# Half of the k-tiles of 25 tile pairs by Strassen's scheme, in a two-layer token-mixing network on one core

## The chip, the core and the metric

The kernel runs on one core of one Trainium2 chip. The metric is the device time of one execution in microseconds (us); less is better. The engines are PE (TensorE, matrix products), DVE (VectorE), ACT (ScalarE), POOL (GpSimd) and SP (SyncE, which starts most DMA transfers). SBUF is the on-chip memory of 128 partitions, PSUM the banks into which PE writes.

## What is computed

Two layers act on x, 512 tokens by 2048 features, in float32. Each is a norm, an input projection, two kinds of mixers over the tokens, and an output projection that is added to x:

```python
def even_layer(x, norm_g, w_in, ...):        # layer 0
    proj = rmsnorm(x, norm_g) @ w_in         # 2048 -> 9 x 1024 + 8 gates
    qa, ka, va, za, qb, kb, vb, ob, zb, gif = split_cols(proj, EV_SIZES)
    ya = chunk_rel_attention(qa, ka, va, ...) * silu(za)            # 8 heads of 128
    yb = sigmoid(ob) * mlstm_chunkwise(qb, kb, vb, li, lf) * silu(zb)   # 4 heads of 256
    return concatenate([ya, yb]) @ w_out
def odd_layer(x, ...):                       # layer 1
    xc, zc, qd, kd, vd, zd, a_pre, b_pre = split_cols(rmsnorm(x, norm_g) @ w_in, OD_SIZES)
    yc = rg_lru(causal_dwconv(xc), ...) * silu(zc)                  # 8 blocks of 128
    yd = rmsnorm(gated_delta_chunkwise(q, k, v, beta, g)) * silu(zd)    # 8 heads of 128
    return concatenate([yc, yd]) @ w_out
for layer in range(2):
    x = x + (even_layer if layer == 0 else odd_layer)(x, ...)
```

## The kernel before

Features lie on the partitions, in 16 k-tiles of 128, and the 512 tokens along the free dimension. Every float32 operand is the sum of a high and a low float32r part, and one product takes three passes (high by high L216, high by low L217, low by high L218), each a matmul of 128x128 weights against 128x512 tokens. One output tile of 128 features is thus 16 k-tiles by 3 passes, 48 matmuls into one of four PSUM banks named `pp`.

`tiles()` cuts an output tile into four units of four k-tiles; `tiles_tok()` makes units of one k-tile for projections that are wanted with tokens on the partitions (the values v), which hold all four `pp` banks at once (L256 to L258). `run()` goes through the units in order. Ahead of unit u it emits the loads up to u + 10 (on SP's queue, into `wr` tiles, of which there are `RAWS` = 4), the splits of the weights up to five units ahead (`AHEAD`; `split_weights`, ACT L185 makes the high part, DVE L186 the low part, into `act` slots, `SLOTS` = 28) and the splits of the operands up to three units ahead (`LEAD`):

```python
while self.nsplit < min(n, u + 1 + AHEAD):
    self.split_weights(self.nsplit)
    self.nsplit += 1
for v in range(u, min(n, u + 1 + LEAD)):
    self.operands(*self.units[v], v == u)
```

The mixers are generators. After every second k-tile `tick()` emits one step of each active one (three in layer 0), and a table of lags `LAG` says how many steps lie between what a mixer orders and what uses it. The order of the instructions on PE, DVE, ACT and POOL is the order in which the program emits them. A finished tile is evicted from PSUM by DVE with the row scale of the norm (L281, L283; L310 and L311 for the token products).

Layer 0 has a first group of five tiles and the gates, which advance together while x arrives (each k-tile of x is split by ACT L354 and DVE L355 or L352, and squared and summed by POOL), then 51 single tiles and four token products, ordered by head: k, q, (v), o, z of the four mLSTM heads, then k, q, (v), z of the eight attention heads (`ATTN_ORDER`), then the 16 output tiles. In an mLSTM head, `pk` holds a matrix of decays that POOL and ACT prepare (L607, L613) and DVE multiplies by the scores from PSUM (L631); POOL adds up its blocks (L634 to L637). The last score block is a product of unsplit operands. In an attention head ACT takes logarithm, exponential and square of the norms (L683, L685, L688, with loads of function tables between), and its last step puts the head's output z into `self.t`, from which the output projection takes it. In layer 1, L1083 and L1080 split the gate weights of a recurrent block.

Of the kernel before, what the change touches and what calls it, by code (L numbers as in the profile page):

```python
# [8 lines left out]
F32 = mybir.dt.float32  # L9
# [7 lines left out]
P = 128  # L17
# [17 lines left out]
# columns of the packed small parameters  # L35
# [28 lines left out]
class Net:  # L64
    """Both layers, features on partitions and tokens along the free dimension.

    Projections: each float32 operand is the exact sum of two float32r parts; a product
    takes three passes (high*high, high*low, low*high). Their weights are streamed in
    pieces of KW k-tiles. The mixers are generators; one step of each active one is
    emitted after every few products of the stream, so that what they wait for is there  # L70
    when the tensor engine comes to them.
    """

    def __init__(self, ctx, tc, a):
# [21 lines left out]
        # the clock of the tensor engine rises after a few microseconds of work  # L96
# [6 lines left out]
        self.t, self.x, self.raw = {}, {}, {}  # L103
        self.heads = 0

# [35 lines left out]
    def tiles(self, specs, group=1):  # L141
        """specs: (weights [P, 16, 128], act, done(psum)); `group` of them advance together.
# [1068 lines left out]
```

## Time and profile before

| | before |
|---|---|
| median of three runs | 1889.77 us (1888.33 to 1890.74) |
| the profiled execution: its span | 1888.7 us |
| PE busy | 1861.9 us, 99% |
| DVE, ACT, POOL busy | 1082.9, 753.1, 254.5 us |

The span of the profiled execution runs from its first to its last instruction; nothing beside the span is recorded of that execution's own time. The busy time of PE counts matmuls that overlap only once, and the mean duration of a matmul is longer than the distance from one to the next.

### The profile page before, as it was taken

To read this page: it belongs to the slowest core of one execution; us is meant where nothing else is said; L and a number is where in the kernel's file an instruction comes from. 1 tells how busy PE (TensorE), PEld (TensorE's weight loads), DVE (VectorE), ACT (ScalarE), POOL (GpSimd) and SP (SyncE) were. 2 spreads that over 40 slices of the span, in tenths; PEclk is the share of its full clock that TensorE was granted. 3 is DMA by queue.
4 is the path that set the end of the run, shared out by engine and by line. 5 is a ranking of instruction groups with operands and counts; after the bars stand their busy time and mean duration, and the time that the engine had idled before them with its cause. 6 is when DMAs were issued, how large, how long until landed. Compare 5 with 4: busy or idle time off the path is not lost.

```text
span 1888.7 us, 24074 instructions
## 1 busy us (share of the span) xinstructions
PE 1861.9 (99%) x8814; PEld 1526.8 (81%) x8814; DVE 1082.9 (57%) x1871; ACT 753.1 (40%) x1311; POOL 254.5 (13%) x298
## 2 busy tenths in 40 slices
PE   7999999999999999999999999999999999999999
PEld 5788888888888888888888788887788877778887
DVE  8564444334443655356643589989756666767222
ACT  4252323223243555355432544363324434566111
POOL 8110000000000011000121113400211112101000
PEclk9999999999999999999999999999999999999999
DMA  5333333333333332332454345433533334235432
GB/s 168 95 113 93 100 104 94 88 104 95 92 85 98 79 95 88 103 85 75 115 174 150 115 121 158 158 106 91 156 96 102 104 96 114 65 95 187 131 115 67
DMA packets 116694, 206.20 MB, mean 109 GB/s; under 512 B 21328, under 2 KB 22480, under 8 KB 116576
## 3 DMA queue, kind: packets, MB, share of 16 engines
q1 hardware_dynamic: 108512, 181.59, 33.8%
q0 software_dynamic: 5760, 18.88, 2.9%
q10 hardware_dynamic: 2304, 4.20, 0.6%
q8 instruction: 69, 1.13, 0.2%
q14 instruction: 49, 0.40, 0.1%
HBM read 189.37 MB, written 15.24 MB: 108 GB/s over the span
## 4 chain that ended last, share of the span: by engine, by line
PE 87%; DVE 8%; issue 2%; DMA 1%; ACT 1%; SPq 1%; DVEq 0%; POOL 0%; ACTq 0%; POOLq 0%
PE pp L216 23%; PE pp L218 23%; PE pp L217 23%; PE pp L256 3%; PE pp L258 3%; PE pp L257 3%; DVE act L186 2%; DVE ev L862 1%; DVE act L939 1%; DVE act L355 1%; DMA ev<-in_xT 1%; SPq L932 0%; PE at_tr L727 0%; PE inv_z L975 0%; ACT act L185 0%
## 5 line engine op out<-in xcount | busy, mean ns | idle before, releaser
L216 PE MATMUL pp<-act,act 128*128 128x512 f32 x2160 | 860.3, 398 | 1.1 <-ACT act L185 0.6
L218 PE MATMUL pp<-act,act 128*128 128x512 f32 x2160 | 846.8, 392 | 11.7 <-DVE act L186 11.5
L217 PE MATMUL pp<-act,act 128*128 128x512 f32 x2160 | 844.8, 391 | 1.6 <-DVE act L355 1.6
L186 DVE TENSOR_TENSOR act<-wr,act 128x512 fp32r<-128x512 f32 x608 | 440.0, 748 | 224.2 <-ACT act L185 223.4
L218 PEld LDWEIGHTS pp<-act,act 128*128 128x128 f32 x2160 | 407.0, 188 | 102.3 <-DVE act L186 15.6
L216 PEld LDWEIGHTS pp<-act,act 128*128 128x128 f32 x2160 | 407.7, 189 | 86.0 <-ACT act L185 2.5
L185 ACT ACTIVATE act<-wr 128x512 fp32r<-128x512 f32 x608 | 355.6, 621 | 302.2 <-DMA wr<-in_wi 117.3
L217 PEld LDWEIGHTS pp<-act,act 128*128 128x128 f32 x2160 | 407.9, 189 | 82.4 <-DVE act L355 3.1
L281 DVE TENSOR_TENSOR ev<-pp,rb 128x512 f32<-128x512 f32 x63 | 43.5, 690 | 154.7 <-PE pp L218 154.6
L256 PE MATMUL pp<-act,act 128*128 128x512 f32 x256 | 101.2, 395 | 0.0
L258 PE MATMUL pp<-act,act 128*128 128x512 f32 x256 | 99.9, 390 | 0.0
L257 PE MATMUL pp<-act,act 128*128 128x512 f32 x256 | 99.8, 390 | 0.0
L862 DVE SCALAR_TENSOR_TENSOR ev<-cv,cst,ev 128x512 f32<-128x512 f32 x96 | 85.3, 889 | 2.3
L456 ACT ACTIVATE tmp<-ev 128x512 f32<-128x512 f32 x56 | 34.8, 622 | 89.7 <-DVE ev L281 73.8
L716 POOL TENSOR_SCALAR pq<-pq,mx 128x512 f32<-128x512 f32 (+3 forms) x32 | 36.4, 1137 | 251.3 <-DVE mx L715 251.2
L800 DVE TENSOR_TENSOR ev<-ev,pp 128x512 f32<-128x512 f32 x16 | 11.0, 688 | 91.2 <-PE pp L218 91.2
L379 ACT ACTIVATE ev<-ev 128x512 fp32r<-128x512 f32 x40 | 25.2, 630 | 92.7 <-DVE ev L694 36.8
L258 PEld LDWEIGHTS pp<-act,act 128*128 128x128 f32 x256 | 48.1, 188 | 10.2
L256 PEld LDWEIGHTS pp<-act,act 128*128 128x128 f32 x256 | 48.1, 188 | 9.5
L257 PEld LDWEIGHTS pp<-act,act 128*128 128x128 f32 x256 | 48.1, 188 | 9.2
L560 ACT ACTIVATE tmp<-ev 128x512 f32<-128x512 f32 x15 | 9.5, 632 | 99.5 <-DVE ev L553 99.5
L553 DVE TENSOR_TENSOR ev<-ev,pp 128x512 f32<-128x512 f32 x16 | 11.0, 688 | 64.6 <-PE pp L218 54.3
(314 smaller groups left out, 1662.7 us busy)
## 6 DMA issues: line engine op xcount, KB each, us to landing
wr<-in_wi SPq DMA_DIRECT2D x416, 256.0 KB
wr<-in_wo SPq DMA_DIRECT2D x128, 256.0 KB
wr<-in_wv SPq DMA_DIRECT2D x64, 256.0 KB
tmp<-rows SPq DMA_DIRECT2D x24, 256.0 KB
ev<-in_xT SPq DMA_DIRECT2D x16, 256.0 KB
ev<-in_xT POOLq DMA_DIRECT2D x16, 256.0 KB, 3.1
x1d<-ev POOLq DMA_DIRECT2D x16, 256.0 KB, 2.3
ev<-x1d POOLq DMA_DIRECT2D x16, 256.0 KB, 4.4
```

Source lines behind the costliest of these rows:

```text
L185: nc.scalar.activation(h, w, AF.Copy)
L186: nc.vector.tensor_tensor(l, w, h.bitcast(F32), ALU.subtract)
L216: nc.tensor.matmul(ps, h[:, j, :], xh, start=k == 0, stop=False)
L217: nc.tensor.matmul(ps, h[:, j, :], xl, start=False, stop=False)
L218: nc.tensor.matmul(ps, l[:, j, :], xh, start=False, stop=k == KT - 1)
L256: nc.tensor.matmul(ps, xh, h, start=k == 0, stop=False)
L257: nc.tensor.matmul(ps, xh, l, start=False, stop=False)
L258: nc.tensor.matmul(ps, xl, h, start=False, stop=k == KT - 1)
L281: self.nc.vector.tensor_tensor(t, ps, self.rb, ALU.mult)
L456: nc.scalar.activation(th, t, AF.Tanh, scale=0.5)
L716: nc.gpsimd.tensor_scalar(s, s, mx[:, 3, b : b + 1], None, ALU.mult)
L862: nc.vector.scalar_tensor_tensor(t, cv[:, j : j + S], self.col(wcol + j), t, ALU.mult, ALU.add)
```

## The change

Of layer 0's 56 plain input tiles, six are now in the first group, and the other 50 form 25 pairs, which the list `STREAM0` orders. A pair takes k-tiles 0 to 7 by the Winograd form of Strassen's scheme and k-tiles 8 to 15 as before. The 2x2 blocks of the scheme are the pair's two output tiles by the even and odd k-tiles (weights), and even and odd k-tiles by the two halves of 256 tokens (x). Seven products of four k-tiles replace eight, so that 84 matmuls of 128x256 stand in place of 48 of 128x512, next to 48 of 128x512 that stay. A pair has eleven units instead of eight:

```diff
+    def pairs(self, specs):
+        for ws, wd, act, done in specs:
+            s = dict(kind="s", ws=ws, w=wd, act=act, done=done)
+            for f in ("1", "6", "7", "5", "2", "3", (0, 0), (0, 4), "4", (1, 0), (1, 4)):
+                self.units.append((s, f))
```

The sums and differences of weights that the scheme wants are made by POOL from the raw tiles ahead of the split (L221, L224), and each of the seven is then split as weights were (ACT L246, DVE L247):

```diff
+    def form(self, s, f):
+        sub = lambda o, x, y: nc.gpsimd.tensor_tensor(o, x, y, ALU.subtract)
+        if f == "6":
+            nc.gpsimd.tensor_tensor(s["a", 1], s["a", 1], s["a", 2], ALU.add)
+            sub(s["a", 0], s["a", 1], s["a", 0])
+        elif f == "7":
+            s["s3"] = self.raw_tile()
+            sub(s["s3"], s["a", 2], s["a", 0])
+            return s["s3"]
+        elif f == "3":
+            sub(s["a", 0], s["a", 3], s["a", 0])
```

The sums of x are made once, for four pairs of k-tiles, by `sums()`, which `operands()` calls when the first pair comes within three units: an ACT copy with the gain (L310), four DVE operations of 128x256 (L315, three L314), an ACT copy of 128x1024 (L320) and a DVE subtraction of 128x1024 (L321).

The partial results are put together in PSUM where the scheme allows it. Units 6 and 5 are followed by an ACT copy of a bank to SBUF (L352, tiles `ee`), unit 3 by three POOL adds of 128x256 (L355). The evictions add these to PSUM by halves: three half-width DVE operations for the first tile of a pair, two full ones for the second (L424 to L433):

```diff
+            if f in "65":
+                e = s["e" + f] = self.ep.tile([P, S], F32, tag="ee", name=self.uid("ee"), bufs=2)
+                nc.scalar.activation(e, ps, AF.Copy)
+            if f == "3":
+                e16, e75 = s["e6"], s["e5"]
+                add = lambda o, x, y: nc.gpsimd.tensor_tensor(o, x, y, ALU.add)
+                add(e75[:, H:], e16[:, :H], e75[:, H:])
+                add(e16[:, :H], e16[:, :H], e16[:, H:])
+                add(e16[:, H:], e16[:, :H], e75[:, :H])
```

A mixer's finished output goes to DRAM by a POOL DMA (`put()`, L492) where the loads have not yet come to the output projection, and SP loads it again. The buffers change; of `pk` and `pq` there is one tile each instead of two, the mLSTM heads take their turns one after the other (`mheads`), and the last mLSTM score block is now a product of split operands:

```diff
-SLOTS = 28
-EVS = 28
-TMPS = 6
-RAWS = 4
+SLOTS = 34
+EVS = 20
+TMPS = 5
+RAWS = 7
+    def put(self, act, k, t):
+        first = next(u for u, (s, _) in enumerate(self.units) if s["act"] == act)
+        if self.ndma < first:
+            self.nc.gpsimd.dma_start(self.yd[k], t)
+            self.spilt.add((act, k))
+        else:
+            self.t[act, k] = t
-                if n > P:
-                    kb, qb = [t[:, j * P : j * P + P] for t in kp[i]], [t[:, j * P :] for t in qp[i]]
-                    self.product(ps[:, :n], kb, qb, start=i == 0, stop=i == 1)
-                else:
-                    nc.tensor.matmul(ps[:, :n], k2[i][:, j * P : j * P + P], q2[i][:, j * P :], start=i == 0, stop=i == 1)
+                kb, qb = [t[:, j * P : j * P + P] for t in kp[i]], [t[:, j * P :] for t in qp[i]]
+                self.product(ps[:, :n], kb, qb, start=i == 0, stop=i == 1)
```

In the whole program there are 1200 matmuls of 128x512 less and 2100 of 128x256 more; POOL has 175 `TENSOR_TENSOR` and 25 DMAs more, SP 25 DMAs more.

Three places show how the order moves. The first is DVE at the end of the first token product; `pp128` is the first bank of the token product before, `pp138` after, and `ml_s` are mLSTM scores. Before:

```order
L814 TENSOR_SCALAR spl_1000<-sm178_997 128x8
L631 TENSOR_TENSOR pk169_942<-pk169_942,ml_s_180_1007 128x512
L186 TENSOR_TENSOR act182_1017<-wr156_885,act182_1017 128x512
L631 TENSOR_TENSOR pk169_942<-pk169_942,ml_s_183_1026 128x384
L631 TENSOR_TENSOR pk169_942<-pk169_942,ml_s_184_1040 128x256
L186 TENSOR_TENSOR act186_1050<-wr163_914,act186_1050 128x512
L311 SCALAR_TENSOR_TENSOR ev188_1057<-pp128_694,rcol_644,act187_1056 128x512
L311 SCALAR_TENSOR_TENSOR ev189_1063<-pp129_695,rcol_644,act187_1056 128x512
```

After, from the last of the four blocks of `sums()`:

```order
L315 TENSOR_TENSOR act200_1091<-tmp199_1089 128x256
L314 SCALAR_TENSOR_TENSOR act200_1091<-ev10_119,cst_77,act200_1091 128x256
L314 SCALAR_TENSOR_TENSOR act200_1091<-ev10_119,cst_77,tmp199_1089 128x256
L314 SCALAR_TENSOR_TENSOR act200_1091<-ev10_119,cst_77,act200_1091 128x256
L321 TENSOR_TENSOR act202_1097<-act200_1091,act201_1096 128x1024
...
L792 TENSOR_TENSOR pk178_1012<-pk178_1012,ml_s_205_1123 128x512
L247 TENSOR_TENSOR act207_1133<-wr162_923,act207_1133 128x512
L792 TENSOR_TENSOR pk178_1012<-pk178_1012,ml_s_208_1142 128x384
L792 TENSOR_TENSOR pk178_1012<-pk178_1012,ml_s_209_1156 128x256
L247 TENSOR_TENSOR act210_1164<-wr172_984,act210_1164 128x512
L468 SCALAR_TENSOR_TENSOR ev212_1171<-pp138_766,rcol_643,act211_1170 128x512
```

The eviction of the token product's first bank (L311, now L468) and the products with the scores (L631, now L792) have four blocks of five operations ahead of them, of which the first rows show the last.

The second is ACT in an attention head, around the logarithm and exponential of the norms. Before:

```order
L185 ACTIVATE act673_3976<-wr655_3891 128x512
L683 ACT_TABLE_LOAD
L683 ACTIVATE ev675_3988<-at_ss_657_3902,bc98_530 128x512
L683 ACTIVATE ev676_3989<-at_ss_674_3985,bc98_530 128x512
L685 ACT_TABLE_LOAD
L685 ACTIVATE ev675_3988<-ev675_3988 128x512
L685 ACTIVATE ev676_3989<-ev676_3989 128x512
L688 ACTIVATE tmp677_3994<-ev675_3988 128x512
L688 ACTIVATE tmp678_3995<-ev676_3989 128x512
L185 ACTIVATE act680_4006<-wr658_3911 128x512
L185 ACTIVATE act682_4026<-wr664_3935 128x512
```

After:

```order
L246 ACTIVATE act888_5649<-wr876_5569 128x512
L845 ACT_TABLE_LOAD
L845 ACTIVATE ev891_5670<-at_ss_874_5548,bc100_534 128x512
L845 ACTIVATE ev892_5671<-at_ss_890_5667,bc100_534 128x512
L847 ACT_TABLE_LOAD
L847 ACTIVATE ev891_5670<-ev891_5670 128x512
L847 ACTIVATE ev892_5671<-ev892_5671 128x512
L850 ACTIVATE tmp893_5676<-ev891_5670 128x512
L850 ACTIVATE tmp894_5677<-ev892_5671 128x512
L246 ACTIVATE act896_5683<-wr866_5494 128x512
L246 ACTIVATE act899_5701<-wr883_5612 128x512
L352 ACTIVATE ee900_5716<-pp897_5686 128x512
```

A copy of a bank of PSUM (L352, from the pair's bank `pp897`) now stands behind the run of table loads and activations and two splits.

The third is POOL in the mLSTM stage; `wr` are raw weights, `ee` the copies from PSUM. Before, what it did for two heads:

```order
L634 COPY tmp194_1087<-pk169_942 128x128
L635 TENSOR_TENSOR tmp194_1087<-pk169_942 128x384
L636 TENSOR_TENSOR tmp194_1087<-tmp194_1087,pk169_942 128x256
L637 TENSOR_TENSOR tmp194_1087<-tmp194_1087,pk169_942 128x128
L607 TENSOR_TENSOR tmp272_1544<-tmp271_1542,tri2_106 128x512
L610 MEMSET pk273_1546 128x128
L634 COPY tmp309_1786<-pk273_1546 128x128
L635 TENSOR_TENSOR tmp309_1786<-pk273_1546 128x384
L636 TENSOR_TENSOR tmp309_1786<-tmp309_1786,pk273_1546 128x256
L637 TENSOR_TENSOR tmp309_1786<-tmp309_1786,pk273_1546 128x128
```

After, what it does for one pair:

```order
L355 TENSOR_TENSOR ee279_1554<-ee272_1514,ee279_1554 128x256
L355 TENSOR_TENSOR ee272_1514<-ee272_1514 128x256
L355 TENSOR_TENSOR ee272_1514<-ee272_1514,ee279_1554 128x256
L224 TENSOR_TENSOR wr276_1535<-wr276_1535,wr277_1537 128x512
L221 TENSOR_TENSOR wr273_1516<-wr276_1535,wr273_1516 128x512
L221 TENSOR_TENSOR wr290_1649<-wr277_1537,wr273_1516 128x512
L221 TENSOR_TENSOR wr273_1516<-wr284_1606,wr273_1516 128x512
L492 DMA yd_101<-ev283_1604 128x512
```

Seven sums and a DMA for each pair stand where POOL had a few operations per head.

## Rows read from the trace of the kernel before

**Rows 1.** The page: span, busy time by engine, PE and DVE in 40 slices (tenths).

```profile
span 1888.7 us, 24074 instructions
PE 1861.9 (99%) x8814; PEld 1526.8 (81%) x8814; DVE 1082.9 (57%) x1871; ACT 753.1 (40%) x1311; POOL 254.5 (13%) x298
...
PE   7999999999999999999999999999999999999999
...
DVE  8564444334443655356643589989756666767222
```

**Rows 2.** Table by stage: window, length, PE, PEld, DVE, ACT, POOL busy (count), PEclk, DMA share, GB/s.

```profile
0.00:100.00 100.00, 86.94 (x364) 63.94 (x365) 71.63 (x72) 38.41 (x58) 47.72 (x39) 0.95 0.42 135
...
200.00:300.00 100.00, 100.00 (x455) 83.36 (x454) 41.85 (x66) 30.14 (x56) 4.73 (x7) 1.00 0.34 99
...
800.00:900.00 100.00, 100.00 (x463) 83.00 (x462) 57.78 (x116) 58.88 (x108) 9.35 (x8) 1.00 0.29 78
...
1100.00:1200.00 100.00, 100.00 (x486) 83.52 (x485) 92.50 (x221) 46.74 (x78) 32.61 (x43) 1.00 0.51 151
...
1300.00:1400.00 100.00, 95.17 (x507) 77.68 (x506) 70.40 (x99) 28.56 (x50) 12.54 (x16) 0.97 0.44 119
```

**Rows 3.** Timeline of PE: start us, us, engine, line, operation, out<-in; a stream of 512-wide products.

```profile
400.12 0.39 PE L216 MATMUL pp<-act,act 128*128 128x512 f32 x1
...
400.80 0.39 PE L216 MATMUL pp<-act,act 128*128 128x512 f32 x1
```

**Rows 4.** Timeline of PE: the first of six 256-wide products and the product behind them.

```profile
574.66 0.28 PE L387 MATMUL at_pv<-ev,act 128*128 128x256 f32 x1
...
575.37 0.40 PE L216 MATMUL pp<-act,act 128*128 128x512 f32 x1
```

**Rows 5.** Groups by line, whole span: count, busy us, mean ns, idle before and its releasers.

```profile
L185 ACT ACTIVATE act<-wr 128x512 fp32r<-128x512 f32 x608 | 355.6, 621 | 302.2 <-DMA wr<-in_wi 117.3 <-DVE ev L800 103.2 <-PE pp L218 42.1
L218 PEld LDWEIGHTS pp<-act,act 128*128 128x128 f32 x2160 | 407.0, 188 | 102.3 <-DVE act L186 15.6
L281 DVE TENSOR_TENSOR ev<-pp,rb 128x512 f32<-128x512 f32 x63 | 43.5, 690 | 154.7 <-PE pp L218 154.6
L1083 DVE TENSOR_TENSOR gl<-gw,gh 128x256 fp32r<-128x256 f32 x8 | 3.3, 418 | 0.0
```

**Rows 6.** DVE groups by line, 100 to 500 us.

```profile
L186 DVE TENSOR_TENSOR act<-wr,act 128x512 fp32r<-128x512 f32 x134 | 87.8, 684 | 42.0 <-ACT act L185 41.9
```

**Rows 7.** POOL groups by line, whole span.

```profile
L561 POOL TENSOR_TENSOR acc<-acc,tmp 128x512 f32<-128x512 f32 x15 | 19.6, 1304 | 0.3
L636 POOL TENSOR_TENSOR tmp<-tmp,pk 128x256 f32<-128x256 f32 x4 | 4.1, 1023 | 3.8 <-DVE pk L631 3.8
```

**Rows 8.** DVE groups by line, 0 to 45 us.

```profile
L355 DVE SCALAR_TENSOR_TENSOR act<-ev,cst,act 128x512 fp32r<-128x512 f32 x16 | 23.7, 1515 | 5.9 <-ACT act L354 5.9
L186 DVE TENSOR_TENSOR act<-wr,act 128x512 fp32r<-128x512 f32 x10 | 15.7, 1589 | 0.4 <-ACT act L185 0.4
```

**Rows 9.** DVE and ACT groups by line, whole span.

```profile
L311 DVE SCALAR_TENSOR_TENSOR ev<-pp,rcol,act 128x512 fp32r<-128x512 f32 x16 | 11.2, 750 | 11.2 <-ACT act L310 11.2
L683 ACT ACT_TABLE_LOAD x8 | 10.3, 1283 | 0.1
L683 ACT ACTIVATE ev<-at_ss,bc 128x512 f32<-128x512 f32 x16 | 10.9, 689 | 5.6 <-PE at_ss L401 5.1
L613 ACT ACTIVATE pk<-tmp,ccol 128x128 f32<-128x128 f32 x16 | 6.2, 388 | 3.6 <-POOL tmp L607 3.6
L1080 ACT ACTIVATE gh<-gw 128x256 fp32r<-128x256 f32 x8 | 3.2, 402 | 0.0
```

**Rows 10.** Table of windows at the start, columns as in rows 2.

```profile
40.00:45.00 5.00, 1.79 (x4) 1.49 (x5) 5.00 (x5) 0.00 (x0) 4.92 (x4) 0.67 0.14 29
45.00:50.00 5.00, 5.00 (x16) 3.88 (x15) 5.00 (x4) 1.46 (x3) 4.84 (x4) 0.64 0.48 159
```

**Rows 11.** Waits of 1190 to 1260 us: who <- for what: us in total, times, longest.

```profile
ACT act L185 <- DMA wr<-in_wi: 7.8, 5, 3.5
```

More of the change, by code (lines that the diff above doesn't have):

```diff
@@ L102, in __init__ @@
         self.jobs, self.active = deque(), []
-        self.t, self.x, self.raw = {}, {}, {}
-        self.heads = 0
+        self.t, self.x, self.raw, self.full, self.xt = {}, {}, {}, {}, {}
+        self.yd = self.dr.tile([KT, P, S], F32, name="yd")
+        self.spilt = set()
+        self.heads = self.mheads = 0
+        self.paired = {"x0"}
     def uid(self, s):
@@ L181, in split_weights @@
             return
-        w = s[k0]
+        w = self.form(s, k0) if isinstance(k0, str) else s[k0]
         t = self.slot(F32R)
@@ L187, in split_weights, with takes @@
         s[k0] = h, l
+    def takes(self, s, k0):
+        act = s["act"]
+        if s["kind"] == "t":
+            return [(act, k0)]
+        if isinstance(k0, str):
+            return [(act, k) for k in range(2 * SP)]
+        k0 = 2 * SP + k0[1] if s["kind"] == "s" else k0
+        return [(act, k) for k in range(k0, k0 + KW)]
     def run(self):
@@ L224, in operands @@
     def operands(self, s, k0, now):
-        act = s["act"]
-        for k in range(k0, k0 + (1 if s["w"].shape[2] > P else KW)):
+        for act, k in self.takes(s, k0):
             while now and (act, k) not in self.x and (act, k) not in self.t:
@@ L231, in operands, with sums @@
                 self.split(act, k, self.t.pop((act, k)), self.col(C_G1 + k) if act == "x1" else None)
+        if isinstance(k0, str) and s["act"] not in self.xt:
+            if all((s["act"], k) in self.x for k in range(2 * SP)):
+                self.xt[s["act"]] = [self.sums(s["act"], j) for j in range(SP)]
+    def sums(self, act, j):
+        nc = self.nc
+        gain = {"x0": C_G0, "x1": C_G1}.get(act)
+        b1, b2 = self.full.pop((act, 2 * j)), self.full.pop((act, 2 * j + 1))
+        if gain is not None:
+            t = self.tmp()
+            nc.scalar.activation(t, b1, AF.Copy, scale=self.col(gain + 2 * j))
+            b1 = t
+        g = 1.0 if gain is None else self.col(gain + 2 * j + 1)
+        f = self.slot().rearrange("p u (i t) -> p (u i) t", t=H)
+        stt = lambda o, x, y: nc.vector.scalar_tensor_tensor(o, x, g, y, ALU.mult, ALU.subtract)
+        nc.vector.tensor_tensor(f[:, 0], b1[:, H:], b1[:, :H], ALU.subtract)
+        stt(f[:, 1], b2[:, H:], f[:, 0])
+        stt(f[:, 2], b2[:, H:], b1[:, H:])
+        stt(f[:, 3], b2[:, :H], f[:, 1])
+        h, l = [self.slot(F32R).rearrange("p u (i t) -> p (u i) t", t=H) for _ in range(2)]
+        nc.scalar.activation(h, f, AF.Copy)
+        nc.vector.tensor_tensor(l, f, h.bitcast(F32), ALU.subtract)
+        return h, l
@@ L487, in layer0 @@
         gates = [(a["wg0"], "x0", self.keep("g0"))]
-        w = iter(range(56))
-        spec = lambda h, n: (a["wi0"][next(w)], "x0", self.evict((h, n), 1.0 / 16 if n[0] == "q" and len(n) > 1 else None))
-        first = [spec(0, n) for n in ("k0", "k1", "q0", "q1")] + [spec(1, "k0")]
-        self.tiles(first + gates, 6)
+        ev = lambda h, n: self.evict((h, n), 1.0 / 16 if n[0] == "q" and len(n) > 1 else 1.0)
+        first = [(a["wi0"][i], "x0", ev(*n)) for i, n in enumerate(FIRST0)]
+        self.tiles(first + gates, len(FIRST0) + 1)
         raw = [self.ev() for _ in range(KT)]
```

176 lines of the change are left out of this document (127 added, 49 removed).

## Prediction

> **What bounds the kernel now.** I read the page first, then a table by stage, then the timeline of TensorE. The page says that PE (TensorE) is busy 99% of the span and that no slice after the first few has it idle, while DVE (VectorE) is busy 57% with two crowded places, at the start and in layer 1 [rows 1]. The table by stage sharpens this [rows 2]: in layer 0's projections PE is at 100.00 of 100 us whether DVE is busy 41.85 (mLSTM) or 57.78 (attention), and even a DVE of 92.50 leaves it at 100.00. Layer 1 is the only later stage that loses PE time (95.17 of 100 at a mean granted clock of 0.97). So in the part that the change rewrites, the time is the number of matmuls times their spacing, and any gain must come from there. Anything else that the change adds costs nothing until PE has to wait for it.
>
> Durations in the page are no spacings, because matmuls overlap. The spacing is read from start to start in the timeline: three 512-wide products take 0.68 us, so 227 ns each [rows 3]; six 256-wide ones take 0.71 us, so 118 ns each [rows 4].
>
> **The change part by part.** One profiled execution carries the prices; its span is 1888.7 us, 1.1 us under the median of the three runs, and I add that back at the end.
>
> *Products.* For a pair, 48 matmuls of 512 columns go and 84 of 256 come (7 products over 4 pairs of k-tiles, 3 passes each); 48 of 512 stay. With the unrounded spacings, 48 x 226.7 ns = 10.88 us against 84 x 118.3 ns = 9.94 us: 0.94 us per pair, for 25 pairs -23.6 us. The saving is thin: spacings of 10.88/84 = 129.5 ns would cancel it. A row that could do so is the weight load, 188 ns of one [rows 5]; if loads did not overlap with each other, a narrow product would take that and the term would be 25 x (84 x 0.188 - 10.88) = +123 us. In rows 4 six narrow products with their own loads hold 118, so I take -23.6.
>
> The Trainium skill, "TensorE: Matmul & The Clock Gate", section "Back-to-back issue gap", speaks against the change: in streams of weight load and matmul it gives 81 ns a matmul at 128 columns and 131 at 512, so narrow products have the worse price per column. A straight line between them gives, as an estimate from that page, 98 ns at 256: 48 x 131 = 6.3 us become 84 x 98 = 8.2 us, 25 x 1.9 = +48 us in place of -23.6. The trace disagrees at both ends of the sum, with 227 and 118 ns for this kernel's products.
>
> *mLSTM scores.* The last block's 8 plain matmuls become 24 of three passes and 128 columns, at most 24 x 118 ns = 2.8 us, less what the eight took: +1 (0 to +3).
>
> *Weight splits.* A pair splits 11 tiles instead of 8 on ACT (621 ns) and DVE (684 without company, below). These lie beside PE's work as long as DVE has room. Per pair before: 8 x 0.684 + 2 x 0.690 = 6.9 us [rows 5, 6]; after: 11 x 0.684 = 7.5, and five eviction operations, three half wide (0.418) and two full (0.69), 2.6: 10.1 us in the pair's new 9.94 + 10.88 = 20.8 us.
>
> *POOL.* A pair brings four 128x512 sums of weights and three 128x256 adds. By 1304 and 1023 ns [rows 7] that is 8.3 us in 20.8, on an engine that was nearly idle there (4.73 and 9.35 of 100 us [rows 2]). It fits on POOL; the cost is to its neighbour. While POOL was busy all the time, DVE's split took 1589 ns; later, with POOL mostly idle, 684 [rows 6, 8]. If every microsecond of POOL blocked DVE for one, the pair would cost DVE 8.3; if none did, nothing. In rows 8 the block is 905 ns beside POOL operations of some 1304, but there DVE always had work; with work three quarters of the time it meets less, and I take half of POOL's time. The Trainium skill, "SBUF — State Buffer", section "SBUF: two separate sides", calls the port pair that the two engines share an exclusive lock which the first holds for its whole instruction, which would be the end where each microsecond blocks one; this trace agrees that the blocking is of the size of an instruction (905 of 1304 ns).
>
> In mLSTM pairs (13), mixers add 41.85 - 4.5 x 6.9 = 11 us per 100, 2.4 per pair: 10.1 + 2.4 + 0.5 x 9.3 = 17.2 of 20.8. PE keeps its cover, except where the seven narrow units, 1.4 us each, come as a burst: they take 9.9 us of PE, and 7 splits (4.8) with four sums of weights in their way. Five units of lead cover that: +1.5 (0 to +6).
>
> In attention pairs (12), mixers take 57.78 - 4.5 x 6.9 = 27 us per 100, 5.9 per pair: 10.1 + 5.9 + 0.5 x (8.3 + 2.0) = 21.2, against 20.8 and about 1 us of PE's attention matmuls. That is 97%, a little above the 92.50 at which PE lost nothing and about the load where it begins to. Besides, ACT's run of two table loads (1283 each) and six activations (about 0.65 each), 6.5 us, stands in its order ahead of two splits and of the first PSUM copy L352, which POOL's adds and both evictions wait for; five narrow units of lead are 7 us, where five wide ones were 13.6. I take 2.7% of 12 x 21.8 us: +7 (0; at most 2 us per pair, +24).
>
> *The sums of x.* They are made once, between the first token product (v) and the first pair. Before, that place on DVE held only the end of the gates and a few products; now four blocks stand there. One block is four 256-wide operations, 0.418 + 3 x 0.47 = 1.83 us (the product-and-subtract form is some 60 ns dearer: 750 against 690), then ACT's copy of 1024 columns, by extension of 402 and 621 about 1.06, for which DVE waits, then its 1024-wide subtraction, by 418 and 684 about 1.22: 4.2 with hand-overs, so 17 us [rows 5, 9]. PE, from the end of the gates' transposes, has 60 matmuls of the token product (13.6) and 24 of mLSTM scores (about 3.7): 17.3 us until the first pair. DVE comes to the sums some 8 us after that point (ACT has seven exponentials of 388 ns, a table load of 1283 and three splits waiting for new sums of weights [rows 9]). It ends the sums at 25, and behind them stand three products with the scores, two splits and the eviction L468 of the token product's first bank, 4.6 us. The pair's first bank of PSUM is freed only by that eviction, since the token product holds all four. So PE waits from 17.3 to about 29.6, 12.3 us. After a shorter gap at the start (1.79 of 5 us busy) the granted clock was 0.67, then 0.64 [rows 10], near the lower level, 1.2 of 2.4 GHz; a few microseconds of it would cost 1 to 2 more. Against this, DVE may come 4 us earlier: +13 (0 to +20).
>
> *First group.* Six tiles instead of five advance with the arrival of x, where PE lacks work because DVE is late (DVE 5.00 of 5, PE 1.79 [rows 10]). The added tile brings PE 2.7 us of work per split of at most 1.59: -2 (-6 to +2).
>
> *Spilled outputs.* 25 writes on POOL's queue and 25 loads on SP's: 25 x 2 x 256 KB over stages with a DMA share of 0.29 to 0.51 [rows 2]. The writes stand in POOL's order behind DVE's last product, ahead of the next pair's sums: 0 (to +2). One mLSTM head at a time moves steps later, not PE's order of need: 0.
>
> *Layer 1* is not rewritten, but has 7 raw weight tiles for 4 and 34 slots for 28, against 20 mixer tiles for 28. In a busy stretch there ACT waited 7.8 us for weights [rows 11]; deeper loads take some of it away, scarcer mixer tiles may add: -3 (-8 to +5).
>
> Sum: -23.6 + 1 + 1.5 + 7 + 13 - 2 + 0 - 3 = -6.1; 1888.7 - 6.1 + 1.1 = **1884 us**. A measurement of this kernel can tell about 0.2%, 3.8 us, from no change: faster is under 1886.0, slower over 1893.6.
>
> **The rivals.**
> *The covers hold* (0.22): DVE reaches the sums early enough and attention pairs lose nothing. Then -23.6 + 1 + 1.5 + 3 (part of the sums) - 5 = -23: 1867. For it: PE at 100.00 beside a DVE of 92.50. Against: the sums are 17 us that nothing had to hide before.
> *DVE and POOL block each other in the attention pairs* (0.25): a new bound in place of PE. Seven new POOL operations per pair, each delaying a DVE operation by up to 905 ns, are 6.3 us; with the 10.1 + 5.9 and the 1 us that POOL's old work costs, 23.3 against PE's 21.8. It decides as soon as DVE's busy time passes PE's in a pair. Its price is 12 x 1.5 = 18, and as much as 24 where the block lands on a late split; for 7 take 24: **1901**. For it: [rows 8]. Against: POOL works less than half of the time, and layer 1 ran at 92.50.
> *Narrow matmuls do not hold 118 ns in long runs* (0.03): the weight load becomes their bound. It decides at a spacing of 129.5 ns; at 153, halfway to the load's 188, the term is 25 x (84 x 0.153 - 10.88) = +49 for -23.6 and the time 1957, at 188 it is 2031. For it: a narrow product lasts less than its weight load. Against: six in a row hold 118 [rows 4]. The rule on the back-to-back gap in the Trainium skill's page "TensorE: Matmul & The Clock Gate" stands on this rival's side.
> *Layer 1 loses by scarcer mixer tiles* (0.08): +8 to +10 for -3, 1896.
> That the change does not do what it says can be set aside: the order of TensorE's program has 1200 wide matmuls less and 2100 narrow more.
>
> **How the numbers follow.** My forecast has 0.42, with its own range 1876 to 1894: 0.25 faster, 0.15 same, 0.02 slower. With the rivals: faster 0.25 + 0.22 = 0.47; same 0.15 + 0.02 (blocking) + 0.02 (layer 1) = 0.19; slower 0.02 + 0.23 + 0.03 + 0.06 = 0.34. The range 1866 to 1908 takes in all but the narrow-matmul case, the ends of the first two rivals and a part of layer 1's, together under 0.2.
>
> **What would show it.** In the changed kernel's profile: narrow products starting every 118 ns; a gap of PE near 100 us, released by a DVE eviction L468, with a fallen clock behind it; four blocks L314 to L321 of about 4.2 us on DVE just ahead; DVE's split L247 at 800 to 1000 ns on average; DVE over 90 of 100 us in the attention stage with PE at 96 to 99. I am wrong if PE has no gap ahead of the first pair, if it waits in every attention pair, or if layer 1 takes another time than before by over 8 us.

## The result and the profile after

The changed kernel takes 1948.97 us (median of four runs, 1945.94 to 1950.10) against 1889.72 before: a ratio of 1.0311 with a 95% interval of [1.0296, 1.0325], 59 us slower. The forecast was 1884, its range 1866 to 1908. The profiled execution took 1949.46 us, with a span of 1947.7.

The page of the changed kernel (span, busy time by engine, then slices of PE, DVE and the granted clock):

```profile
span 1947.7 us, 26612 instructions
...
PE 1870.5 (96%) x9722; PEld 1572.9 (81%) x9722; DVE 1221.7 (63%) x2041; ACT 817.3 (42%) x1444; POOL 467.2 (24%) x498
...
PE   7997999999999889998899999999899999999999
...
DVE  8467665466655656566653379989946566767322
...
PEclk8997999999999899999999999999999999999999
```

Against [rows 1] PE has two new dents, one in the fourth slice and one from the fourteenth to the twentieth, and DVE is nowhere full in them. (The 8 of the 29th slice is a gap of layer 1 that was there before, 95.17 of 100 us in [rows 2].) The table by stage says where (columns as in [rows 2]):

```profile
100.00:200.00 100.00, 86.12 (x446) 74.80 (x445) 68.78 (x107) 47.83 (x85) 23.70 (x26) 0.90 0.26 80
200.00:600.00 400.00, 400.00 (x2334) 355.64 (x2333) 241.27 (x361) 158.98 (x294) 129.40 (x124) 1.00 0.32 101
600.00:1000.00 400.00, 366.73 (x1986) 317.56 (x1985) 243.57 (x458) 200.25 (x379) 117.65 (x111) 0.94 0.31 95
1000.00:1850.00 850.00, 836.25 (x4186) 683.13 (x4185) 578.04 (x1018) 359.83 (x604) 148.68 (x199) 1.00 0.42 130
```

From 200 to 600 us PE never waits. These are the mLSTM pairs and, from about 510 us on, the first two attention pairs, beside which few attention steps run yet (the first transposes of a softmax start at 567 us). From 600 to 1000, called the attention stage below (the other ten attention pairs and the first output tiles), PE is idle for 33.3 us and its clock is granted 0.94 on average, while DVE is busy 243.57 of 400 us. In the kernel before, PE has no idle time from 600 to 1000 us:

```profile
600.00:1000.00 400.00, 400.00 (x1838) 331.74 (x1837) 212.15 (x419) 188.88 (x355) 53.12 (x59) 1.00 0.36 102
```

From 1000 us on (the last output tiles of layer 0, then layer 1) little has changed. What ACT waited for on POOL's sums, and what PE waited for, in the attention stage (engine, line, releaser: us in total, times, longest; 600 to 1000 us):

```profile
ACT act L246 <- POOL wr L221: 28.2, 9, 5.4
...
PE at_tr L889 <- DVE ev L894: 11.8, 4, 4.9
...
PE at_ss L568 <- DVE mx L874: 5.8, 2, 2.9
...
PE pp L336 <- ACT ee L352: 4.4, 2, 2.2
...
PE at_sc L555 <- ACT ev L547: 3.9, 1, 3.9
```

PE never waits for a split of weights here (for splits of operands, L519 and L520, 2.6 us). It waits above all for the mixers: for PSUM banks that the transposes of the softmax (`at_tr`) need and that DVE L894 frees, for the bank of the sums of squares (`at_ss`), and also for a copy L352; most of these waits are 2 to 5 us long. All small products of the mixers share four PSUM banks, so that a bank of one head that is read late holds up another head's products. The stalls do not end with the wait: the first of these windows holds one of them, the others lie behind it:

```profile
666.00:676.00 10.00, 6.70 (x31) 5.39 (x30) 4.48 (x7) 7.23 (x12) 4.46 (x4) 0.84 0.14 51
676.00:680.00 4.00, 4.00 (x23) 3.50 (x22) 2.77 (x7) 1.26 (x2) 1.29 (x1) 0.88 0.00 0
680.00:684.00 4.00, 4.00 (x19) 3.29 (x18) 3.31 (x6) 1.35 (x3) 0.00 (x0) 1.00 0.00 0
```

PE has worked without a pause since 672.25 us, and still its granted clock is 0.88 from 676 to 680 us, a mean of its two levels, 1.2 and 2.4 GHz. So in that stage idle time and slow clock both count.

Two waits read on ACT's timeline show the two ways in which it is late. In the first, ACT has made two of four copies of a head's transposes (L892); then come the table loads and activations of the next head's norms (L845, L847, L850), and only behind them the other two copies:

```profile
663.46 0.27 ACT L892 ACTIVATE ev<-at_tr 128x128 fp32r<-128x128 f32 x1
...
664.17 0.38 ACT L892 ACTIVATE ev<-at_tr 128x256 fp32r<-128x256 f32 x1
664.56 1.28 ACT L845 ACT_TABLE_LOAD   x1
665.85 1.27 ACT L845 ACTIVATE ev<-at_ss,bc 128x512 f32<-128x512 f32 x2
667.14 1.28 ACT L847 ACT_TABLE_LOAD   x1
668.43 1.15 ACT L847 ACTIVATE ev<-ev 128x512 f32<-128x512 f32 x2
669.49 1.13 ACT L850 ACTIVATE tmp<-ev 128x512 f32<-128x512 f32 x2
...
671.05 0.47 ACT L892 ACTIVATE act<-at_tr 128x384 fp32r<-128x384 f32 x1
```

On PE, the fourth transposes start at 672.25, after 3.30 us of waiting. The run splits the four copies of three heads in this way; PE waits in two of them (3.34 us in the other, to 894.22), and not in the third, near 758 us, beside a token product. In the second, ACT stands at a weight split for 5.39 us, and the copies L892 are next in ACT's order:

```profile
708.41 0.63 ACT L246 ACTIVATE act<-wr 128x512 fp32r<-128x512 f32 x1 [5.39 <-POOL wr L221]
708.95 0.29 ACT L883 ACTIVATE ev<-ident 128x128 fp32r<-128x128 f32 x1
709.15 0.53 ACT L892 ACTIVATE ev<-at_tr 128x128 fp32r<-128x128 f32 x2
```

On POOL the sums of weights that ACT waits for come behind the adds L355, and those behind the softmax products (L878), which wait for DVE:

```profile
702.27 0.60 POOL L878 TENSOR_SCALAR pq<-pq,mx 128x128 f32<-128x128 f32 x1 [1.23 <-DVE mx L877]
702.84 0.98 POOL L355 TENSOR_TENSOR ee<-ee,ee 128x256 f32<-128x256 f32 x1
...
707.12 2.61 POOL L221 TENSOR_TENSOR wr<-wr,wr 128x512 f32<-128x512 f32 x2
```

and PE starts its transposes 4.89 us late:

```profile
712.21 1.11 PE L889 MATMUL at_tr<-ident,pq 128*128 128x128 f32 x4 [4.89 <-DVE ev L894]
```

### The profile page after: what moved, and what is told of

Its sections match the earlier page's. It is cut to its first block, busy times and chain, and to the rows that moved or that the text cites. A ratio compares the mean times of both kernels' runs of the same rounds, so it can differ in the third digit from the quotient of the medians.

```text
span 1947.7 us, 26612 instructions
## 1 busy us (share of the span) xinstructions
PE 1870.5 (96%) x9722; PEld 1572.9 (81%) x9722; DVE 1221.7 (63%) x2041; ACT 817.3 (42%) x1444; POOL 467.2 (24%) x498
## 4 chain that ended last, share of the span: by engine, by line
PE 73%; DVE 13%; ACT 6%; issue 5%; DMA 2%; POOL 1%; SPq 1%; DVEq 0%; ACTq 0%; POOLq 0%
PE pp L336 21%; PE pp L284 12%; PE pp L286 12%; PE pp L285 12%; DVE act L247 4%; PE pp L398 3%; PE pp L400 3%; PE pp L399 3%; ACT act L246 2%; DVE ev L1024 1%; DVE act L1101 1%; DMA ev<-in_xT 1%; ACT pq L876 1%; DVE ev L626 0%; SPq L1094 0%
## 5 line engine op out<-in xcount | busy, mean ns | idle before, releaser
L247 DVE TENSOR_TENSOR act<-wr,act 128x512 fp32r<-128x512 f32 x683 | 535.7, 808 | 307.8 <-ACT act L246 305.4
L336 PE MATMUL pp<-act,act 128*128 128x256 f32 (+1 forms) x3300 | 554.9, 329 | 15.6 <-DVE ev L468 11.0
L336 PEld LDWEIGHTS pp<-act,act 128*128 128x128 f32 x3300 | 494.2, 196 | 67.3 <-DVE ev L468 11.4
L284 PE MATMUL pp<-act,act 128*128 128x512 f32 x1344 | 541.0, 402 | 3.1 <-ACT act L519 2.2
L286 PE MATMUL pp<-act,act 128*128 128x512 f32 x1344 | 528.4, 393 | 9.5 <-DVE act L247 9.2
L285 PE MATMUL pp<-act,act 128*128 128x512 f32 x1344 | 527.0, 392 | 2.1 <-DVE act L523 1.7
L246 ACT ACTIVATE act<-wr 128x512 fp32r<-128x512 f32 x683 | 394.8, 619 | 290.1 <-POOL wr L221 129.4
L286 PEld LDWEIGHTS pp<-act,act 128*128 128x128 f32 x1344 | 253.9, 189 | 67.4 <-DVE act L247 13.2
L284 PEld LDWEIGHTS pp<-act,act 128*128 128x128 f32 x1344 | 254.6, 189 | 57.3 <-issue 3.0
L285 PEld LDWEIGHTS pp<-act,act 128*128 128x128 f32 x1344 | 254.4, 189 | 52.9 <-DVE act L523 3.1
L221 POOL TENSOR_TENSOR wr<-wr,wr 128x512 f32<-128x512 f32 x75 | 98.7, 1316 | 65.0 <-issue 33.4
L398 PE MATMUL pp<-act,act 128*128 128x512 f32 x256 | 102.0, 398 | 3.0 <-DVE ev L429 3.0
L400 PE MATMUL pp<-act,act 128*128 128x512 f32 x256 | 100.7, 393 | 0.0
L399 PE MATMUL pp<-act,act 128*128 128x512 f32 x256 | 100.4, 392 | 0.0
L492 POOL DMA_DIRECT2D yd<-ev x25 | 14.4, 577 | 303.7 <-DVE ev L1232 94.7
L355 POOL TENSOR_TENSOR ee<-ee,ee 128x256 f32<-128x256 f32 x50 | 44.9, 898 | 172.6 <-ACT ee L352 159.2
L878 POOL TENSOR_SCALAR pq<-pq,mx 128x512 f32<-128x512 f32 (+3 forms) x32 | 34.9, 1093 | 179.6 <-DVE mx L877 179.4
L962 DVE TENSOR_TENSOR ev<-ev,pp 128x512 f32<-128x512 f32 x16 | 11.0, 687 | 91.9 <-PE pp L286 91.9
L398 PEld LDWEIGHTS pp<-act,act 128*128 128x128 f32 x256 | 48.5, 189 | 13.1 <-DVE ev L429 3.4
L624 ACT ACTIVATE tmp<-ev 128x512 f32<-128x512 f32 x56 | 34.9, 622 | 54.5 <-DVE ev L431 32.4
```

The costliest lines, as they stand in the source:

```text
L221: sub = lambda o, x, y: nc.gpsimd.tensor_tensor(o, x, y, ALU.subtract)
L246: nc.scalar.activation(h, w, AF.Copy)
L247: nc.vector.tensor_tensor(l, w, h.bitcast(F32), ALU.subtract)
L284: nc.tensor.matmul(ps, h[:, j, :], xh, start=k == 0, stop=False)
L285: nc.tensor.matmul(ps, h[:, j, :], xl, start=False, stop=False)
L286: nc.tensor.matmul(ps, l[:, j, :], xh, start=False, stop=k == KT - 1)
```

## The experiments

Sixteen kernels were run. Times of single gaps in the expectations are by the trace's own clock, on which the span begins at 10.5 us; the rows count from the span's start. The theories: A, POOL's sums of weights are late and hold up ACT; B, the PSUM copies do; C, the added splits do; D, the order in which the tiles of a pair arrive; E, the place of one head's run of table loads among another head's copies (the expectation of e9 calls it theory C in its sharper form). Beside the edits shown, e4 and e10 to e13 have EVS 22 and SLOTS 33; e7 and e8 have SLOTS 33, RAWS 8 and three `ee` tiles.

**e3, the sums of x early.** They are made in the last round of the first group.

```diff
-        if isinstance(k0, str) and s["act"] not in self.xt:
-            if all((s["act"], k) in self.x for k in range(2 * SP)):
-                self.xt[s["act"]] = [self.sums(s["act"], j) for j in range(SP)]
+        if s["act"] == "x0" and s["kind"] == "w" and k0 == 12 and s["i"] < SP:
+            xt = self.xt.setdefault("x0", [])
+            if len(xt) == s["i"]:
+                xt.append(self.sums("x0", s["i"]))
```

> The changed kernel with the four blocks of sums of x emitted in the last round of the first group, where DVE has little to do, instead of ahead of the first pair. If these sums alone make PE wait there: the gap of 11.1 us at 155 us and the slow clock behind it go, and the time falls by 13 to 20 us, 1929 to 1936 us. Rival (the wait only moves, or another late step of that place takes its place): less than 8 us, over 1941 us.

1935.6 us, 13.4 less. The wait of 11.0 us for L468 is gone, and the stage from 100 to 200 us reads

```profile
100.00:200.00 100.00, 96.70 (x531) 84.37 (x530) 67.10 (x100) 46.97 (x88) 28.89 (x29) 0.98 0.29 89
```

**e4, pairs in the mLSTM stage alone.** The 24 attention tiles are dense.

```diff
-        STREAM0.append(("p", [(_h, _s[0]), (int(_s[3]), _s[2])]))
+        STREAM0.append(("d", [(_h, _s[0]), (int(_s[3]), _s[2])]))
```

> Only the 13 pairs of the mLSTM stage take the scheme, the 24 attention tiles are dense as before (EVS 22, SLOTS 33). If a pair is worth 0.9 us where PE has no wait, the sums of x still cost some 19 us and the attention stage loses nothing: 1889.7 - 12 + 1 + 19 = 1898 us, 1893 to 1903. If the attention stage's loss came from the buffers or the serial heads and not from the pairs: 1940 us or more.

1900.3 us, within the forecast range; from 600 to 1000 us PE is busy 400.00 of 400. The loss of the attention stage comes with its pairs, not with the buffers or the serial heads (e10 below has the same EVS and SLOTS as e4, and the attention pairs, and keeps the loss).

**e1, without POOL's sums of weights.**

```diff
-            nc.gpsimd.tensor_tensor(s["a", 1], s["a", 1], s["a", 2], ALU.add)
-            sub(s["a", 0], s["a", 1], s["a", 0])
...
-            sub(s["s3"], s["a", 2], s["a", 0])
...
-            sub(s["a", 0], s["a", 3], s["a", 0])
```

> The changed kernel without POOL's four sums of weights per pair (they are left out of the computation, raw weights are split in their place). Theory A (POOL's sums are late in the attention stage, behind the softmax products and the adds on POOL; ACT stands at the split of such a sum, and the mixers' steps behind it on ACT and DVE come late, so PE waits and its clock falls): most of the some 58 us that PE loses between 640 and 1000 us is gone, 1900 to 1915 us. Theory B (the PSUM copies on ACT, or the shorter lead of five narrow units, hold the mixers up, whatever POOL does): 1935 to 1950 us. The gap of 11 us ahead of the first pair stays in both.

1928.6 us, 20 less: between the two theories. A is a part, not most of it. The edit takes away the late sums and also what POOL's work costs DVE (the split L247 takes 811 ns on average in the attention stage of the changed kernel, 779 here); it does not tell the two apart.

**e2, the adds on DVE.**

```diff
-                add = lambda o, x, y: nc.gpsimd.tensor_tensor(o, x, y, ALU.add)
+                add = lambda o, x, y: nc.vector.tensor_tensor(o, x, y, ALU.add)
```

> The changed kernel with the three adds of 128x256 per pair on DVE instead of POOL. Theory A (POOL's queue is what is late): POOL is relieved of about 2.7 us a pair and of its wait for the PSUM copies, so the sums of weights come earlier: 1915 to 1940 us. Theory B (copies or lead): no gain, 1945 to 1955 us, and DVE gets 1.3 us per pair more.

1947.7 us, no gain that can be told. Taking 2.8 us per pair off POOL does not bring the sums in time: from 600 to 1000 us ACT waits for them 27.4 us, and 28.2 in the changed kernel.

**e5, without the copies and adds** (the branches `if f in "65"` and `if f == "3"` go, and the evictions add `self.rb`).

> The changed kernel without the two PSUM copies on ACT and the three POOL adds per pair (left out of the computation; the evictions add another tile in their place). Without POOL's sums the loss fell by 20 us of some 58, and PE then still waited for a copy (two gaps of 3.7 us) and for transposes. Theory B (PE's next write to the bank waits for the copy, which stands on ACT behind the softmax): those gaps go, 1915 to 1930 us. Theory A alone (POOL's sums): 1940 us or more, since moving the adds away gained 1 us.

1934.3 us, 15 less; a little short of what B alone would give.

**e6, without both** (the edits of e1 and e5).

> Both left out: POOL's four sums of weights, and the PSUM copies and adds. If sums and copies are the whole of the attention stage's loss: 1893 to 1905 us, with the 16 us at the first pair still in. Theory C (the shorter lead: splits come every 1.4 us in the narrow units, so that DVE and ACT are late with the mixers by themselves): over 1912 us, with PE still waiting for transposes and at the end of the attention stage.

1916.0 us, 33 less than the changed kernel: the two causes about add up (20 + 15), and something else remains. Waits of PE for copies are gone, those for transposes are not:

```profile
PE at_tr L874 <- DVE ev L879: 10.3, 4, 4.4
```

**e7, the last two dense units of a pair behind the next pair's first two.**

```diff
-            for f in ("1", "6", "7", "5", "2", "3", (0, 0), (0, 4), "4", (1, 0), (1, 4)):
-                self.units.append((s, f))
+            self.units += [(s, "1"), (s, "6"), *self.late]
+            self.units += [(s, f) for f in ("7", "5", "2", "3", (0, 0), (0, 4), "4")]
+            self.late = [(s, (1, 0)), (s, (1, 4))]
```

> The last two dense units of a pair come behind the first two narrow units of the next (three ee tiles, RAWS 8, SLOTS 33), so that the first copy of a pair has 8 us until PE writes to its bank again, where it had 2.8. Theory B: the waits of PE for the copy go (2 to 4 us of gaps, each with a slow clock behind it), and the mixers' results come more evenly: 1930 to 1942 us. Theory A or C: 1944 to 1955 us.

1961.7 us, 13 more, outside the ranges of all the theories. The copies have time now (no wait for L352 is left), but PE waits 22.5 us for `at_tr` where it waited 11.8. The edit moved the mixers' steps as well; that this is what cost more was not tried by itself.

**e8, e7 with POOL's sums earlier and the sums of x early** (the sums are made up to two units ahead of the splits; the first product thereby takes a sum in place of its raw tile).

> The order of e7 with POOL's sums emitted one unit earlier than their splits need them and the sums of x emitted in the first group. If the three causes add up: 13 us from the sums of x, 8 from the copies, 10 to 20 from the sums of weights, 1905 to 1920 us. If one unit of lead for POOL's sums is not worth anything: 1925 to 1935 us.

1941.0 us, 21 less than e7, of which 13 are the sums of x by e3. It lies outside both ranges and tells little, since e7's loss is in it.

**e9, a lag of 7 for `at.ss`, on e3.**

```diff
-    "at.ss": 4, "at.sc": 5, "at.tr": 3, "at.pv": 7,
+    "at.ss": 7, "at.sc": 5, "at.tr": 3, "at.pv": 7,
```

> The kernel of e3 (1935.6 us) with the lag at.ss 7 instead of 4: a head's sums of squares, and with them ACT's run of two table loads and six activations, come six steps (some 8 us) later. Theory C in its sharper form (that run stands on ACT ahead of the copies that free the PSUM banks of the head before, for which PE's transposes wait): the gaps ahead of transposes at 664, 703 and 886 us go, 1920 to 1928 us. If the run is not what holds them: 1933 to 1940 us.

1933.7 us: no difference beyond the runs' spread (1932.2 to 1935.2). In ACT's rows the run now stands behind all four copies in every head, and PE's waits for transposes fall from 13.0 us in e3 to 8.0; but those for copies stay (10.5, in e3 9.4) and 6.5 for evictions L469 come. Moving the run alone, with the steps that hang on it, gained nothing.

**e10, another order of the attention pairs, on e3.**

```diff
-for _s in "k0q0 v0 z0k1 q1z1 k2q2 z2k3 q3z3 k4q4 v4 z4k5 q5z5 k6q6 z6k7 q7z7".split():
+for _s in "k0q0 v0 k1q1 z0z1 k2q2 k3q3 z2z3 k4q4 v4 k5q5 z4z5 k6q6 k7q7 z6z7".split():
```

> The kernel of e3 with the attention pairs in another order: k and q of one head in a pair, z of two heads in a pair, so that the last pair is z6z7 (EVS 22, SLOTS 33). If the order in which the tiles arrive makes the waits: the gaps at the end of the attention stage (from 944 us, some 9 us with the slow clock behind them) go, and those of the heads 0 and 4 change place: 1915 to 1928 us. If it is the density of small work per pair, whatever the order: 1932 to 1942 us.

1936.8 us, no difference that can be told (the two runs: 1933.4 and 1940.2); the waits moved to the sums of squares (15.9 us for L564).

**e11, only z in pairs in the attention stage**, with early sums of x, by `"k0 q0 v0 k1 q1 z0z1 k2 q2 k3 q3 z2z3 ..."`.

> Early sums of x; the 13 mLSTM pairs and four pairs of z tiles take the scheme, k and q of the attention heads are dense single tiles. By e4 (1900.3) less 13.4 for the early sums less 4 x 0.9: 1883 us, 1881 to 1887, if the z pairs make nothing wait; over 1890 if any pair in the attention stage does.

1908.5 us: a miss by 25. Four pairs are enough to make PE wait 10.2 us for transposes, twice 5.1. Here it is not the copies that free the bank late but DVE L860, which reads a sum of squares and stands behind the same run of ACT (from 677.24 to 683.30 us, L860 at 685.20, the transposes at 685.94).

**e12, only the mLSTM pairs, with early sums of x** (e3 and e4 together).

> Early sums of x; only the 13 mLSTM pairs take the scheme. e4 less what e3 gained: 1900.3 - 13.4 = 1887 us, 1885 to 1889, a little under the kernel before (1890).

1885.7 us in 11 runs, a ratio of 0.9976 [0.9967, 0.9984]: it beats the kernel before, by 4 us. From 200 to 1000 us PE is busy 800 of 800. The spacing of its 13 pairs saves 10.4; a part of that is lost from 100 to 200 us, where PE is busy 97.58 and was 100.00.

**e13, dense tiles in the order in which a pair's tiles arrive**, on e12.

```diff
+                two = [dict(kind="w", ..., i=0) for t in b[1]]
+                self.units += [(two[i], k) for i, k in ((0, 0), (1, 0), (0, 4), (1, 4), (0, 8), (0, 12), (1, 8), (1, 12))]
```

> The kernel of e12 (1885.7 us) with the attention tiles still dense, but two of them advancing together in the order of the changed kernel's pairs, so that they end 5.4 us apart; no narrow products, no sums, no copies, no added splits in that stage. Theory D (the order in which tiles arrive lets the run of ACT of one head meet the transposes of the other): over 1893 us, up to 1910, with PE waiting for transposes near 660 and 870 us. Theory C (added splits at a higher rate): 1884 to 1888 us.

1888.7 us. D by itself costs 3 us, not 30 (runs of 1886.7 to 1891.1, those of e12 1882.6 to 1887.9); the row of the stage is

```profile
600.00:1000.00 400.00, 399.01 (x1831) 330.59 (x1830) 211.83 (x417) 186.28 (x353) 54.44 (x63) 1.00 0.38 113
```

**e14, four splits in the narrow part instead of seven, on e6.**

```diff
+        if k0 in ("6", "5", "3"):
+            s[k0] = s["kept"]
+            return
```

> The kernel of e6 (1916.0 us, no sums of weights, no copies) with four splits per pair in the narrow part instead of seven (units 6, 5 and 3 take the parts of the unit before them, which is left out of the right computation), so that a pair has eight splits as before the change. Theory C (added splits): PE's loss between 640 and 1000 us falls from 36 to under 15 us, 1890 to 1897 us. Theory D (order of arrival): 1908 to 1918 us.

1911.0 us, 5 less (two runs each; those of e6 lie 4.4 apart): C is at most a small part. With no sums, no copies and no added splits, PE still waits twice some 5 us for transposes (9.9 us in all, 2 times, by the waits), and ACT's rows show again the run with its two table loads ahead of the third copy, in both places:

```profile
646.28 1.28 ACT L833 ACT_TABLE_LOAD   x1
...
652.77 0.47 ACT L880 ACTIVATE act<-at_tr 128x384 fp32r<-128x384 f32 x1
...
653.98 1.12 PE L877 MATMUL at_tr<-ident,pq 128*128 128x128 f32 x4 [4.96 <-DVE ev L882]
```

That left the places in the order. A pair calls `tick()` once in each of its seven narrow units and twice in its four dense ones, 15 times, where two tiles called it 16 times.

**e15, the sixteenth step given back, on e3.**

```diff
+            if f == "4":
+                self.tick()
```

> The kernel of e3 (1935.6 us) with a second step of the mixers in unit 4 of a pair, so that a pair gives them 16 steps as two tiles did before, where the change gives 15. In the order on ACT, the run of two table loads and six activations of a head's norms then stands behind the last of the four copies of the transposes of the head before (L892), where in the changed kernel it stands between the second and the third of three heads. Theory E (that place in the order makes PE wait for the run, 6.5 us, since the banks of the transposes come free only behind it): the gaps at 664 and 886 us go and their slow clock, 1915 to 1924 us. If the lost step is not what moves the waits: 1932 to 1938 us.

1920.2 us, 15 less. The four copies now stand ahead of the run:

```profile
643.81 0.26 ACT L895 ACTIVATE ev<-at_tr 128x128 fp32r<-128x128 f32 x1
...
644.49 0.38 ACT L895 ACTIVATE ev<-at_tr 128x256 fp32r<-128x256 f32 x1
...
645.75 0.50 ACT L895 ACTIVATE act<-at_tr 128x384 fp32r<-128x384 f32 x1
...
646.64 0.62 ACT L895 ACTIVATE act<-at_tr 128x512 fp32r<-128x512 f32 x1
647.28 1.28 ACT L848 ACT_TABLE_LOAD   x1
```

and PE's wait for transposes falls to 2.8 us, from 13.0 in e3 (the first line); its two waits behind the run, 3.82 us to 657.76 and 4.03 to 880.11 in e3, are 0.17 each. What is left is above all the wait for copies:

```profile
PE at_tr L890 <- DVE ev L895: 13.0, 4, 4.9
...
PE pp L337 <- ACT ee L353: 11.4, 4, 4.6
...
PE at_tr L892 <- DVE ev L897: 2.8, 3, 2.5
```

**e16, the same step on e6.**

> The kernel of e6 (1916.0 us; no sums of weights, no copies) with the same second step in unit 4. Theory E: its two gaps of 4.5 us ahead of transposes, at 663 and 871 us, and what the clock loses behind them go, 1898 to 1906 us; what then stays is the end of the attention stage and the token products. If not: 1913 to 1918 us.

1901.9 us, 14 less than e6, and PE's wait for transposes falls from 10.3 us to 5.2. So the missing step is worth 15 us with all of the change's work and 14 with none of its sums and copies.

In both, the run of ACT no longer stands among the copies of any head; the two waits that stood behind it are 0.17 us each in e15, and in e16 2.6 each, in e6 4.3. But the step moves everything that the mixers do, and e9, which moved the run alone, gained nothing. So the price of the step is shown; that it works by the place of the run is read from the rows for these waits, and for the rest of its gain it is likely but not shown.

## Why the prediction was wrong

*Products.* The mechanism was right and the size nearly so. From 302.71 us the changed kernel ran 2 wide products, 72 narrow ones and a wide one without a pause:

```profile
302.71 9.48 PE L336 MATMUL pp<-act,act 128*128 128x512 f32 x75
```

Less 0.45 us for the first two and 0.39 for the last, 8.64 us for 72 narrow products are 120 ns each, where 118 was taken: 0.80 us per pair (10.88 against 10.08) instead of 0.94, -20 for 25 pairs instead of -23.6. The rival that narrow products slow down would have given 1957 and comes nearest to the time, but the rows exclude it. (Its reason misread [rows 4]: what is below the weight load's 188 ns is the spacing of narrow products, 118; one lasts 280.) A time that fits is no proof of its mechanism. The figures of the Trainium skill's "TensorE: Matmul & The Clock Gate", section "Back-to-back issue gap", 131 ns at 512 columns and by the prediction's estimate 98 at 256, are not those of this stream either, which has 227 and 120.

*mLSTM scores.* +1 forecast; by the rows around 143 us, and around 132 before, a head's last block takes some 0.2 us more, 0.8 for four.

*Sums of x.* Right, in size and mechanism: 13.4 us by e3, +13 forecast. A block took 0.42 + 3 x 0.48 on DVE, 1.06 on ACT and 1.22 on DVE, by these rows, and the wait was 11.0 us (12.3 forecast) with a granted clock of 0.50 in the window around it:

```profile
L321 DVE TENSOR_TENSOR act<-act,act 128x1024 fp32r<-128x1024 f32 x4 | 4.9, 1225 | 4.7 <-ACT act L320 4.7
L320 ACT ACTIVATE act<-act 128x1024 fp32r<-128x1024 f32 x4 | 4.2, 1058 | 9.3 <-DVE act L314 6.9 <-PE pp L400 2.4
L314 DVE SCALAR_TENSOR_TENSOR act<-ev,cst,act 128x256 f32<-128x256 f32 x8 | 3.9, 481 | 0.1
...
L315 DVE TENSOR_TENSOR act<-tmp 128x256 f32<-128x256 f32 x4 | 1.7, 420 | 0.0
...
148.00:160.00 12.00, 3.72 (x17) 3.72 (x18) 10.14 (x21) 5.98 (x11) 4.37 (x5) 0.50 0.10 26
```

*mLSTM pairs.* +1.5 forecast, nothing measured: 400.00 of 400.

*Attention pairs.* This step failed: "I take 2.7% of 12 x 21.8 us: +7 (0; at most 2 us per pair, +24)". Between e3 and e12 the 12 pairs cost 49.9 us although their products saved 12 x 0.80; so the stage lost some 59. I sized it by DVE's load, 21.2 us per pair, 97%. DVE was busy 243.57 of 400 us, 61%, and no bound: the rival of DVE and POOL blocking each other fell too. One term of that load can be read by itself. I let POOL's work cost DVE half of POOL's time. From 200 to 600 us the changed kernel has DVE busy for 241.27 us beside 129.40 of POOL, and e6, with as many DVE operations (364, here 361), for 216.23 beside 22.90 (its row is at the end), which is 0.24 us per us.

But no load was the cause. PE never waited for a split of weights. It waited mostly for mixer steps that came late because their engines, ACT above all, stood before them at something else in their order. I had noted the run of ACT ahead of a copy but priced it against the lead of the splits, not against the PSUM banks of another head's transposes.

The parts, by what came back when each was taken out: POOL's sums 20 (e1), copies and adds 15 (e5), both 33 (e6), the missing step 15 (e15 against e3) or 14 (e16 against e6), added splits 5 (e14 against e6), the order of the tiles 3 (e13 against e12). They overlap and need not add up exactly. With sums, copies and the missing step put aside, 59 - 33 - 14 leaves 12 us; what e16 still loses was not split further.

*First group, layer 1.* -2 forecast; the first token product starts at 97.15 us and started at 86.10, which is the sixth tile's own 48 products at 227 ns (10.9) and nothing gained. -3 forecast; from the last write of layer 0's output (L718, before L554) to the end it is 819.0 us (from 1128.7) and was 816.6 (from 1072.1), so the deeper buffers gave nothing.

The terms as measured, -20 + 0.8 + 0 + 59 + 13.4 + 0.2 + 2.4, make 56 of the 59 us. A wait of 2.9 us behind the first pair (to 176.12 us, for DVE L565), which the prediction does not have, is about the rest.

## What to carry to other kernels

In a stream whose order is written out with fixed lags, a change of the number of steps per unit of work is a change of its own: count the steps, and look for where a long run on one engine lands among the instructions that free the buffers another engine waits for. Average load does not show such waits; read the order of the engine that frees the bank. Where a scheme saves 7% on a part of the products, put it first where the mixers have slack, and try each stage by itself: the 13 pairs of the quiet stage gained, the 12 of the busy one cost, on balance, five times what their products saved (50 us for 9.6).

## What was unexpected of the hardware

A wait of a few microseconds can be paid twice. In the attention stage the waits alone, 33.3 us, are less than the some 59 that it lost; a mean clock of 0.94 over 400 us is up to 24 more. A short wait can do it too: in e16 PE waited for 2.15 us, and behind it, without a pause, it ran at 0.50, its lower level (behind another, of 2.61 us to 853.00, it stayed at 1.00 until 860):

```profile
896.16 0.64 PE L556 MATMUL at_ss<-tmp,ones_r 128*128 128x512 f32 x1 [2.15 <-DVE tmp L552]
...
897.00:899.00 2.00, 2.00 (x6) 1.59 (x5) 0.90 (x2) 1.98 (x3) 0.00 (x0) 0.50 0.29 60
```

And POOL's 128x512 sums took 1316 ns, the 1304 of [rows 7], while DVE's split went from 686 ns on average to 825 from 200 to 600 us: DVE is the one that gives way. (The lines: DVE's split there before and after; the row of e6, where POOL does little and the split takes 702 ns; POOL's sums over the whole span.)

```profile
L186 DVE TENSOR_TENSOR act<-wr,act 128x512 fp32r<-128x512 f32 x136 | 89.1, 686 | 47.9 <-ACT act L185 47.9
...
L247 DVE TENSOR_TENSOR act<-wr,act 128x512 fp32r<-128x512 f32 x179 | 142.7, 825 | 98.2 <-ACT act L246 97.9
...
200.00:600.00 400.00, 400.00 (x2357) 356.71 (x2356) 216.23 (x364) 149.69 (x272) 22.90 (x32) 1.00 0.34 103
...
L221 POOL TENSOR_TENSOR wr<-wr,wr 128x512 f32<-128x512 f32 x75 | 98.7, 1316 | 65.0 <-issue 33.4 <-DVE act L247 14.1 <-POOL wr L221 10.9
```
